# Down projections of an MLP as seven products of half blocks per pair of output tiles, in a two-layer streaming encoder on one core

## The chip, the cores and the metric

The kernel runs on one core of a Trainium2 chip. A core has five engines that work at the same time, each through its own queue of instructions, in order: TensorE (PE) multiplies matrices, VectorE (DVE), ScalarE (ACT) and GpSimd (POOL) work on elements, and SyncE (SP) issues DMAs. ACT and POOL can issue DMAs too. They share an on-chip memory, SBUF, of 128 partitions; TensorE writes its results to the banks of a second memory, PSUM, from where the others read them. An instruction waits at the head of its queue until the data that it reads is there and the buffer that it writes is free, and what stands behind it waits with it.

The metric is the time of one execution on the device in microseconds (us), the median over several runs.

## The reference

One inference step on T = 576 tokens: 512 of a new stream and 64 of a running one. The model has a width of 1024 and two layers. Layer 0 mixes tokens with causal means over windows, layer 1 with sparse attention: an indexer scores the keys, the best are chosen, and attention runs over these. Each layer ends in an MLP of 4096 hidden features, and normalisation by the root of the mean square stands ahead of each part:

```python
def _mlp(h, w_up, w_down):
    u = jax.nn.relu(h @ w_up)
    return (u * u) @ w_down

x = x + y.astype(x.dtype)
x = x + _mlp(_rmsnorm(x, norm_mlp[i]), mlp_w_up[i], mlp_w_down[i])
```

All is 32-bit floating point. The two MLPs have most of the multiplications: `w_up` is 1024 x 4096, `w_down` 4096 x 1024.

## The kernel before, in words

**Layout.** Activations lie with features on the partitions and tokens along the free axis. The residual stream `x` is eight tiles of 128 features by 576 tokens. A matmul takes a 128x128 block of weights, loaded into TensorE first (PEld in the profile), and streams tokens past it, half of them (`HT` = 288) at a time.

**Three passes.** Each float32 operand is taken apart into an upper part that TensorE takes as `fp32r` and a lower part, the rest. A product is then upper by upper, upper by lower and lower by upper: three matmuls in place of one. `project` (L151, the matmul at L159) does this for one output tile of 128 features: for each of eight k tiles, three passes over two halves of tokens, so 48 matmuls into two banks of PSUM.

**Weights.** They come as blocks of 128x1024, one for each output tile, in a list `blocks` in the order of use. `next_block` (L135) keeps two blocks ahead: it loads a block by a DMA on ACT's queue (`load`, L107; two raw tiles), and `split_weights` (L112) lets ACT write the upper part (L115) and DVE the lower one (L116) into one of three pairs of weight tiles.

**The MLP.** `mlp` (L245) takes the hidden features in four chunks of 1024. A chunk has an up stage of eight output tiles and a down stage of eight. After each up tile `squared` (L250) makes the factor of the down stage: DVE takes relu times 1/rms out of PSUM (L252), ACT squares (L253), and `split` makes the upper part on ACT (L145) and the lower on DVE (L146). A down tile sums over the eight factors of its chunk, and DVE adds it to the residual (L277). The last three tiles of the last chunk of layer 1 are done by `last` (L281) in two parts of the tokens, so that the final norm of the one runs beside the products of the other; this part alone has TensorE's order written out by hand.

**Norms.** `Norm` squares each tile of x on ACT, sums on DVE, and `stats` and `spread` sum over partitions by matmuls on TensorE (`st` in the profile, then `rb`, after a diagonal that DVE makes at L202). At the start of attention `split_x` (L236) makes the split activations `xs` of attention from x, tile by tile, and the norm's sums with them. The first products of attention are `ki` (the indexer's keys) and `pj` (projections, rotated by `rope`); `ki` is read by DVE at L609 and L610 once 1/rms is spread, since cosine and sine carry it.

**Order.** Outside of `last` a scheduler in the compiler of the kernel places the instructions on each engine, by the dependencies and by a model of the times. It may move the work of one stage beside that of another.

**Dependencies.** An engine waits for another by the tiles that both touch: a PSUM tile of two banks, as `ps` gives out (three buffers of them; `po` has two of one bank), is one tile for these waits.

## Time and profile before

| | |
|---|---|
| time, median of 3 runs | 1177.26 us (1177.13 to 1177.45) |
| the profiled execution: its span | 1175.3 us |
| TensorE matmuls busy, number | 1143.3 us, 97% of the span, 8580 |
| DVE busy | 595.4 us, 51% |
| ACT busy | 437.1 us, 37% |
| POOL busy | 169.1 us, 14% |
| DMA, mean over the span | 99 GB/s |

The span is the time from the first to the last instruction that the profiler recorded in one execution; the runs' time has about 2 us around it. Busy time is counted per engine. The page then shows the chain of work that ended last, followed back from the last instruction to what released it, step by step; groups of like instructions, with the busy time, the mean duration of one, and the idle time of the engine before them with what ended it; and the DMA issues with the median time from issue to landing. In a row `out<-in` names the tiles, `x384` counts instructions, and L159 is a line of the kernel. Two other views are rows in order of time (start, duration, engine, line) and tables of stretches of time (each engine's busy time, the clock that TensorE was granted, the share of the DMA engines, GB/s).

### The profile page before, as it was taken

The page shows a single profiled execution, that of the slowest core. Times are in us where ns is not written, and L with a number is a line of the kernel's source. Part 1 is how long each engine was busy: PE and PEld are TensorE (multiplying, and loading weights), DVE is VectorE, ACT ScalarE, POOL GpSimd, SP SyncE. Part 2 cuts the span into 40 slices and gives each one's busy share as a digit, 9 for nine tenths or more (in the row PEclk, how much of TensorE's full clock was granted, in tenths as well). Part 3 has the DMA queues.
Part 4 walks back from the last instruction along what each step waited for, and adds up shares of the span by engine and source line. Part 5 has one row for each costly group of instructions (what it writes and reads, how often), then busy time and mean ns, then how long its engine had stood idle before and what let it go on. Part 6 is the DMA issues. An engine that isn't in the chain of part 4 may idle for free.

```text
span 1175.3 us, 20225 instructions
## 1 busy us (share of the span) xinstructions
PE 1143.3 (97%) x8580; PEld 1130.9 (96%) x8580; DVE 595.4 (51%) x1000; ACT 437.1 (37%) x713; POOL 169.1 (14%) x125
## 2 busy tenths in 40 slices
PE   7999999999999999998889999999999999999996
PEld 6999999999999999998879999999999999999995
DVE  7844234333333445869999943753343334324444
ACT  5633123123212433344377665542133123213331
POOL 7600000000000000227874430000000000000002
PEclk8999999999999999999989999999999999999998
DMA  6222222222222233456452341422322222222212
GB/s 208 60 90 72 90 84 79 91 74 89 87 76 90 75 128 121 149 175 185 144 159 75 119 126 45 150 74 89 87 76 91 76 87 90 73 90 80 84 55 81
DMA packets 51146, 116.64 MB, mean 99 GB/s; under 512 B 9345, under 2 KB 22960, under 8 KB 51056
## 3 DMA queue, kind: packets, MB, share of 16 engines
q10 hardware_dynamic: 23184, 84.45, 23.2%
q1 hardware_dynamic: 27872, 30.90, 8.6%
q8 instruction: 67, 1.10, 0.4%
q14 instruction: 23, 0.19, 0.0%
HBM read 99.73 MB, written 13.25 MB: 96 GB/s over the span
## 4 chain that ended last, share of the span: by engine, by line
PE 90%; DVE 6%; ACT 1%; issue 1%; DMA 1%; SPq 0%; DVEq 0%; ACTq 0%
PE up L159 35%; PE dn L159 34%; PE pj L159 5%; PE o L798 2%; PE wa L159 2%; PE wo L159 2%; DVE work L723 1%; PE sc L759 1%; PE pt L779 1%; PE v L915 1%; PE pb L548 1%; DVE m L722 1%; DVE wl L116 1%; PE o L802 1%; PE z L441 1%
## 5 line engine op out<-in xcount | busy, mean ns | idle before, releaser
L115 ACT CAST wh<-raw 128x1024 fp32r<-128x1024 f32 (+1 forms) x161 | 168.8, 1049 | 603.9 <-PE dn L159 299.3
L159 PE MATMUL dn<-u,wh 128*128 128x288 f32 (+2 forms) x2048 | 358.2, 296 | 0.0
L159 PE MATMUL up<-xs,wh 128*128 128x288 f32 x2048 | 356.3, 296 | 0.0
L159 PEld LDWEIGHTS dn<-u,wh 128*128 128x128 f32 x2048 | 301.3, 188 | 0.2
L159 PEld LDWEIGHTS up<-xs,wh 128*128 128x128 f32 x2048 | 300.1, 188 | 0.2
L159 PE MATMUL dn<-u,wl 128*128 128x288 f32 (+2 forms) x1024 | 222.9, 295 | 0.0
L159 PE MATMUL up<-xs,wl 128*128 128x288 f32 x1024 | 219.0, 295 | 0.0
L116 DVE TENSOR_TENSOR wl<-raw,wh 128x1024 fp32r<-128x1024 f32 (+1 forms) x149 | 186.3, 1250 | 30.4 <-ACT wh L115 23.0
L277 DVE TENSOR_TENSOR x<-x,dn 128x576 f32<-128x576 f32 x61 | 46.0, 754 | 245.5 <-PE dn L159 245.5
L159 PEld LDWEIGHTS dn<-u,wl 128*128 128x128 f32 x1024 | 165.8, 188 | 0.0
L159 PEld LDWEIGHTS up<-xs,wl 128*128 128x128 f32 x1024 | 164.4, 188 | 0.1
L252 DVE SCALAR_TENSOR_TENSOR v<-up,rbm 128x576 f32<-128x576 f32 x64 | 48.3, 757 | 204.9 <-PE up L159 204.3
L159 PE MATMUL pj<-xs,wh 128*128 128x288 f32 x448 | 79.5, 296 | 0.0
L305 POOL TENSOR_TENSOR x<-x,rb 128x320 f32<-128x320 f32 (+1 forms) x9 | 7.9, 908 | 454.7 <-ACT rb L301 454.7
L159 PEld LDWEIGHTS pj<-xs,wh 128*128 128x128 f32 x448 | 66.5, 188 | 0.6
L606 POOL TENSOR_TENSOR cs<-cs,rba 128x576 f32<-128x576 f32 x1 | 1.9, 1862 | 415.2 <-ACT rba L190 415.2
L146 DVE TENSOR_TENSOR u<-v,u 128x576 fp32r<-128x576 f32 x64 | 48.4, 758 | 13.3 <-ACT u L145 13.2
L159 PE MATMUL pj<-xs,wl 128*128 128x288 f32 x224 | 48.4, 295 | 0.0
L738 ACT ACTIVATE p<-p,nm 128x128 f32<-128x128 f32 (+4 forms) x72 | 41.9, 584 | 10.4 <-DVE nm L737 10.1
L253 ACT ACTIVATE v<-v 128x576 f32<-128x576 f32 x64 | 43.9, 687 | 2.4 <-DVE v L252 1.9
L145 ACT CAST u<-v 128x576 fp32r<-128x576 f32 x64 | 43.1, 676 | 1.9
L798 PEld LDWEIGHTS o<-V,pT 128*128 128x128 f32 x320 | 40.2, 196 | 1.9 <-ACT pT L780 1.5
(191 smaller groups left out, 1215.4 us busy)
## 6 DMA issues: line engine op xcount, KB each, us to landing
raw<-in_w_up ACTq DMA_DIRECT2D x64, 512.0 KB, 3.6
raw<-in_w_down ACTq DMA_DIRECT2D x64, 512.0 KB, 3.5
raw<-in_w_o ACTq DMA_DIRECT2D x16, 512.0 KB, 3.6
raw<-in_w_in ACTq DMA_DIRECT2D x15, 512.0 KB, 3.9
q<-st SPq DMA_DIRECT2D x32, 144.0 KB, 2.5
q<-q SPq DMA_DIRECT2D x16, 256.0 KB, 2.8
x<-in_x SPq DMA_DIRECT2D x8, 288.0 KB, 5.9
xd<-x SPq DMA_DIRECT2D x4, 576.0 KB, 2.8
```

The costliest lines, as they stand in the source:

```text
L115: (act.copy if top is act else top.tensor_copy)(h[:, :n], raw[:, :n])
L116: sub.tensor_tensor(l[:, :n], raw[:, :n], f32(h[:, :n]), ALU.subtract)
L145: act.copy(dst[:, 0], src)
L146: sub.tensor_tensor(dst[:, 1], src, f32(dst[:, 0]), ALU.subtract)
L159: pe.matmul(pt[:, h, :m], wt[:, k * P:(k + 1) * P], xs[k][:, part, c:c + m], start=(k == 0 and i == 0), stop=(k == n - 1 and i == 2),)
L252: dve.scalar_tensor_tensor(halves(v), pt[:, :, :HT], 0.0, halves(norm.rb), ALU.max, ALU.mult)
L253: act.activation(v, v, AF.Square)
L277: dve.tensor_tensor(halves(x[m]), halves(x[m]), pt[:, :, :HT], ALU.add)
L441: pe.matmul(z[s, i][:n, (g % 2) * 256:(g % 2 + 1) * 256], lhs, rhs, start=kk + j == 0, stop=kk == 1 and j == 2)
L548: pe.matmul(pt[:, c0:c0 + rhs.shape[1]], lhs, rhs, start=n == 0, stop=n == len(steps) - 1)
L738: act.activation(dst, dst, AF.Exp, scale=-1.0, bias=nm, accum_out=sums)
L798: pe.matmul(oc[:, 2 * s + hh], pT[:, c:c + P], V[:, kt, vs], start=kt == 0, stop=kt == i)
```

## The change

The down stages of all four chunks of layer 0 and of the first three of layer 1 take two output tiles at a time and compute them by Strassen's scheme in Winograd's form. The two output tiles by two halves of k make a 2x2 block matrix of weights, a11 to a22 (128x512 each in the layout of the blocks), and the two halves of k by two halves of tokens one of factors, b11 to b22. Eight products of such blocks become seven, of weights a11, a12, a22 and four sums of weights with b11, b21, b22 and four sums of factors (t1 to t4). Each product is 12 matmuls: four k tiles, three passes, one half of the tokens.

- **Weights.** Blocks and pairs stand in one list `jobs`, and the generator `made` yields units of 128x512, upper and lower part each; an ordinary block is two units. There are six unit tiles, and two more (`more`) during the MLPs, every fourth unit from those two. Of a pair both blocks are loaded whole into `pair` tiles (one pair's worth of buffers). The sum s1 comes by a plain load of a quarter and an accumulating DMA on POOL's queue, the sum with a21 by another such DMA into the raw tile; the two values of s2 come by POOL additions. `next_unit` keeps four more units ahead.
- **Factors.** After two up tiles (the order of the up tiles, `UP_ORDER`, pairs k with k + 4) `factors` makes four sums on DVE and splits seven factors in four wide instructions.
- **Products.** `Pair` has banks a and b, halves of one PSUM tile, and c, a tile by itself. Three products open the pair, each into a bank of its own; four more go on accumulating into a, b, c and b, and after each DVE adds that bank to the residual (the line after `product` in `closing`). The first product, a11 by b11, is needed in all four outputs: it is summed over the chunks in `part_sums` and added on POOL in the last Strassen chunk.
- **Order.** TensorE's order in both MLPs is that of the source (`manual_schedule`); the first up tile of the next chunk stands ahead of a down stage. In the first pair of a chunk the last quarter of the three opening products runs after the first three quarters of all three.
- **Memory.** Tile pools that were there for the whole kernel are now opened for each stage (`stage`).

The pool mixer's weights and the value projection's are cut into units as well. The core of the diff:

```diff
-SLOTS = {"x": 4, "xs": 8, "a": 3, "b": 3, "c": 3, "d": 3, "e": 2}
+SLOTS = {"xs": 8, "a": 3, "b": 3, "c": 3, "d": 3, "e": 2}
+UNITS = 6
+UP_ORDER = (0, 4, 1, 5, 2, 6, 3, 7)
+FACTORS = ("b11", "b22", "b21", "t1", "t2", "t3", "t4")
...
-    weights = ctx.enter_context(tc.tile_pool(name="weights", bufs=3))
+    weights = ctx.enter_context(tc.tile_pool(name="weights", bufs=UNITS))
...
+    @contextmanager
+    def stage(**pools):
+        with ExitStack() as st:
+            phase.clear()
+            for name, bufs in pools.items():
+                phase[name] = st.enter_context(tc.tile_pool(name=uid(name), bufs=bufs, reuse_waits="tile"))
+            yield
...
+    def mlp_jobs(layer, strassen):
+        for c in range(4):
+            ups = [("block", a["w_up"][layer, c * 8 + f], KT * P) for f in UP_ORDER]
+            jobs.extend(ups[1:] if c else ups)
+            if c < 3:
+                jobs.append(("block", a["w_up"][layer, (c + 1) * 8 + UP_ORDER[0]], KT * P))
+            if c < strassen:
+                jobs.extend(("pair", a["w_down"][layer, c, 2 * q], a["w_down"][layer, c, 2 * q + 1]) for q in range(KT // 2))
+            else:
+                jobs.extend(("block", a["w_down"][layer, c, m], KT * P) for m in range(KT))
...
+    def unit(n=512):
+        extra = phase.get("more")
+        count[0] += 1
+        if extra and made_units[0] % 4 == 3:
+            got = [extra.tile([P, 528], F32R, tag=t, bufs=2, name=uid(t)) for t in ("wh", "wl")]
+        else:
+            got = [weights.tile([P, 528], F32R, tag=t, name=uid(t)) for t in ("wh", "wl")]
+        made_units[0] += 1
+        return [t[:, :n] for t in got]
...
+    def split_unit(src, n=512):
+        h, l = unit(n)
+        act.copy(h, src)
+        how["sub"].tensor_tensor(l, src, f32(h), ALU.subtract)
         return h, l
...
+    def made():
+        while jobs:
+            kind, one, two = jobs.pop(0)
+            if kind == "block":
+                raw = load(one, two, act)
+                for i in range(2):
+                    yield split_unit(raw[:, i * two // 2:(i + 1) * two // 2], two // 2)
+                continue
+            r = [phase["pairs"].tile([P, KT * P], F32, tag="pair", bufs=2, name=uid("pair")) for _ in range(2)]
+            for t, src in zip(r, (one, two)):
+                act.dma_start(t, src)
+            a11, a12, a21, a22 = (t[:, i * 512:(i + 1) * 512] for t in r for i in range(2))
+            s1, s2 = (phase["pairs"].tile([P, 512], F32, tag="sum", bufs=4, name=uid("sum")) for _ in range(2))
+            act.dma_start(s1, two[:, :512])
+            pool.dma_start(s1, two[:, 512:], accum_op=ALU.add)
+            pool.dma_start(a21, one[:, :512], accum_op=ALU.add)
+            pool.tensor_tensor(s2, s1, a11, ALU.add)
+            yield split_unit(a11)
+            yield split_unit(s2)
+            yield split_unit(s1)
+            yield split_unit(a12)
+            yield split_unit(a21)
+            pool.tensor_tensor(s2, s2, a12, ALU.add)
+            yield split_unit(s2)
+            yield split_unit(a22)
...
+    def next_unit(ahead=4, sub=dve):
+        how["sub"] = sub
+        while len(ready) <= ahead:
+            u = next(units, None)
...
+        return ready.pop(0)
...
+        def factors(v):
+            t = phase["acts"].tile([P, 4, HT], F32, tag="t", bufs=1, name=uid("t"))
+            u = phase["u"].tile([P, 7, 2, HT], F32R, tag="u", bufs=4, name=uid("u"))
+            b12, b11, b22, b21 = (v[:, i] for i in range(4))
+            act.copy(u[:, 0:3, 0], v[:, 1:4])
+            dve.tensor_tensor(t[:, 0], b11, b12, ALU.subtract)
+            dve.tensor_tensor(t[:, 1], b22, t[:, 0], ALU.add)
+            dve.tensor_tensor(t[:, 2], b12, b22, ALU.subtract)
+            dve.tensor_tensor(t[:, 3], b21, t[:, 1], ALU.subtract)
+            act.copy(u[:, 3:7, 0], t)
+            dve.tensor_tensor(u[:, 0:3, 1], v[:, 1:4], f32(u[:, 0:3, 0]), ALU.subtract)
+            dve.tensor_tensor(u[:, 3:7, 1], t, f32(u[:, 3:7, 0]), ALU.subtract)
             return u
...
+        def product(bank, w, us, factor, js, first, last):
+            for j in js:
+                wh, wl = (t[:, j * P:(j + 1) * P] for t in w)
+                uh, ul = (us[j][:, FACTORS.index(factor), i] for i in range(2))
+                for i, (wt, ut) in enumerate(((wh, uh), (wh, ul), (wl, uh))):
+                    pe.matmul(bank[:, :HT], wt, ut, start=first and j == 0 and i == 0, stop=last and j == 3 and i == 2,
+                              skip_group_check=True)
...
+                ab = psum("ab")
+                self.a, self.b, self.c_ = ab[:, 0], ab[:, 1], psum1("c")
+                self.lo, self.hi = ([x[2 * q + i][:, c0:c0 + HT] for i in range(2)] for c0 in (HT, 0))
...
+            def opening(self, parts=((0, 1, 2, 3),)):
+                ws = [next_unit() for _ in range(3)]
+                for js in parts:
+                    for w, bank, factor in zip(ws, (self.a, self.b, self.c_), ("b11", "t2", "t1")):
+                        product(bank, w, self.us, factor, js, True, True)
+                    yield
+                self.opened()
...
+            def opened(self):
+                q = self.q
+                if self.c == 0:
+                    part_sums[q] = phase["acts"].tile([P, HT], F32, tag=f"g{q}", bufs=1, name=uid("g"))
+                    act.copy(part_sums[q], self.a[:, :HT])
+                else:
+                    dve.tensor_tensor(part_sums[q], part_sums[q], self.a[:, :HT], ALU.add)
+                dve.tensor_tensor(self.hi[0], self.hi[0], self.b[:, :HT], ALU.subtract)
+                dve.tensor_tensor(self.hi[1], self.hi[1], self.c_[:, :HT], ALU.subtract)
+                if self.c == strassen - 1:
+                    g = part_sums[q]
+                    pool.tensor_tensor(self.hi[0], self.hi[0], g, ALU.add)
+                    pool.tensor_tensor(self.hi[1], self.hi[1], g, ALU.subtract)
+                    pool.tensor_tensor(self.lo[1], self.lo[1], g, ALU.subtract)
...
+            def closing(self):
+                js = (0, 1, 2, 3)
+                for bank, factor, out, b2 in ((self.a, "b21", self.lo[0], 0), (self.b, "t3", self.hi[1], 0),
+                                              (self.c_, "b22", self.hi[0], 0), (self.b, "t4", self.lo[1], 0)):
+                    product(bank, next_unit(), self.us, factor, js, False, True)
+                    dve.tensor_tensor(out, out, bank[:, :HT], ALU.add)
...
+        def down(c, us):
+            for q in range(KT // 2):
+                p = Pair(c, q, us)
+                for _ in p.opening(((0, 1, 2, 3),) if q else ((0, 1, 2), (3,))):
+                    pass
+                p.closing()
...
+        steps = [s for c in range(4) for s in [(c, i) for i in range(c > 0, 8)] + ([(c + 1, 0)] if c < 3 else []) + [(c, None)]]
+        for n, (c, i) in enumerate(steps):
+            if i is not None:
+                w = next_block(sub=add if n < 2 else dve)
                 pt = psum("up")
                 project(pt, w, xs)
...
+            if c < strassen:
+                down(c, us[c])
+                continue
...
-    pool_mixer()
-    mlp(0, 1, ["xs"] * KT, "abcdabcdabcd", pool)
-    attention()
-    mlp(1, 3, "aaabbbcc", ["xs"] * KT + ["c", "d", "d", "d"], end=last)
+    x = Residual()
+    with stage(slots=1, xs=1, tmps=6):
+        pool_mixer()
+    with stage(u=1, xs=1, acts=1, tmps=3, pairs=1, more=2):
+        with tc.manual_schedule(engines={ENG.PE}):
+            mlp(0, 1, 4, pool)
+    with stage(slots=1, xs=1, cst2=1, tmps=6):
+        attention()
+    with stage(xs=1, u=1, acts=1, tmps=3, pairs=1, more=2):
+        with tc.manual_schedule(engines={ENG.PE}):
+            mlp(1, 3, 3, end=last)
```

More of the change, by code (lines that the diff above doesn't have):

```diff
@@ L1 @@
-from contextlib import ExitStack
+from contextlib import ExitStack, contextmanager
 import numpy as np
@@ L126, in pool_dsa_kernel @@
[L126 to L140 removed]
+    jobs = []
@@ L532, in pool_mixer @@
             dve.tensor_copy(sband, sraw)
-            src, n = blocks.pop(0)
-            split_blocks.append(split_weights(load(src, n, act), n, act, pool))
+            how["sub"] = pool
+            for _ in range(2):
+                ready.append(next(units))
         two = psum("z")
```

155 lines of the change are left out of this document (87 added, 68 removed).

## The prediction

> **What bounds the kernel now.** I read the page first: busy time, chain, groups.
>
> ```profile
> span 1175.3 us, 20225 instructions
> PE 1143.3 (97%) x8580; PEld 1130.9 (96%) x8580; DVE 595.4 (51%) x1000; ACT 437.1 (37%) x713; POOL 169.1 (14%) x125
> PE 90%; DVE 6%; ACT 1%; issue 1%; DMA 1%; SPq 0%; DVEq 0%; ACTq 0%
> L115 ACT CAST wh<-raw 128x1024 fp32r<-128x1024 f32 (+1 forms) x161 | 168.8, 1049 | 603.9 <-PE dn L159 299.3
> ```
>
> TensorE is 97% busy and makes 90% of the chain; ACT's idle time is waiting for TensorE. Then the chain in order of time, where the down and up stages stand as unbroken pieces:
>
> ```profile
> 101.84 50.96 PE dn L159 x384
> 152.80 51.01 PE up L159 x384
> 458.68 6.39 PE ki L159 x48
> 465.19 0.99 PE st L209 x10
> 466.19 6.46 PE pj L159 x47
> 472.64 0.97 PE rb L189 x4
> ```
>
> A down stage is 384 matmuls in 50.96 us, 132.7 ns each, without a gap, and attention's first products follow without one. In the MLP the time is the number of matmuls; anything that makes TensorE wait there is added to the span. The table of stretches for a down stage says what room the others have:
>
> ```profile
> 100.00:150.00 50.00, 50.00 (x379) 50.00 (x378) 16.60 (x17) 9.76 (x10) 0.00 (x0) 1.00 0.26 78
> ```
>
> DVE is a third busy, ACT a fifth, POOL idle, the granted clock full.
>
> The profiled span is 1175.3 us and the runs' median 1177.3; I carry the 2.0 us around the span through unchanged and make the sum on the span.
>
> **What is removed.** A pair of output tiles takes 96 matmuls now (2 tiles x 8 k x 3 passes x 2 halves), 84 as seven products of 12. Four chunks of layer 0 and three of layer 1, four pairs each: 28 x 12 = 336 matmuls less, x 132.7 ns = **-44.6 us**. All matmuls of a product go to one bank; that costs nothing by the attention's output products, which do so already:
>
> ```profile
> 636.55 2.85 PE wa L159 x24
> ```
>
> 24 of 256 columns in 2.85 us are 119 ns, 107 of streaming and 12 over; 132.7 for 288 columns is 120 and 12.7.
>
> **New waits of TensorE inside a pair.** The products run a(b11), b(t2), c(t1), a(b21), b(t3), c(b22), b(t4); call them 1 to 7. Banks a and b are halves of one tile, and the changed program waits by tile: product 5 starts only when DVE has read a after product 4, and nothing stands between the two. Product 4 waits in the same way for DVE's reading of b after product 2; product 7 for that of product 5, with product 6 between. The price of such a wait is the drain, the reading, and the restart:
>
> ```profile
> 394.56 0.43 PE L159 MATMUL up<-xs,wl 128*128 128x288 f32 x2
> 394.82 0.56 PE L159 MATMUL up<-xs,wh 128*128 128x288 f32 x3
> 395.02 0.76 DVE L252 SCALAR_TENSOR_TENSOR v<-up,rbm 128x576 f32<-128x576 f32 x1 [3.41 <-PE up L159]
> L327 DVE TENSOR_TENSOR x<-x,dn x6: 407/455/489, 1144.1 to 1162.1; 128x320 f32<-128x320 f32 x3, 128x256 f32<-128x256 f32 x3
> 8.79 1.23 DVE L417 TENSOR_TENSOR wl<-raw,wh 128x1024 fp32r<-128x1024 f32 x1 [1.38 <-ACT wh L414]
> 10.07 0.19 PEld L441 LDWEIGHTS z<-wl,xs 128*128 128x128 f32 x1 [0.48 <-DVE wl L417]
> ```
>
> The next block's first matmul takes its place at 394.82, DVE reads the old one at 395.02: 0.20. Reading 128x288 lies between the 407 and 489 ns of 256 and 320 columns: 0.45. DVE ends at 10.02, the weight load starts at 10.07, its matmul some 0.04 later: 0.09. Together 0.74 us before product 5 of every pair. In the last pair of layer 0 the scheduler has put attention's products into the gaps, so 27 x 0.74 = **+20.0**. Bounds: 0, if the reading were somehow covered, and 27 x 1.2 = 32, if DVE is late by one subtraction.
>
> Before product 4 the readings of a and b (0.45 each) have one product, 1.59 us, to hide under in an ordinary pair. Not in the first pair of a chunk, where the last quarter of products 1 to 3 runs together: 0.8 us in five chunks. In each layer's first chunk ACT copies a, behind the copy of a weight, and DVE's reading of b stands behind it (in the first pair behind a subtraction and c's reading too): about 1.9 us in its first pair, 0.4 in the three others. 5 x 0.8 + 2 x 1.9 + 6 x 0.4 = **+10.2** (0 to 15).
>
> **Engines beside it.** Weights are split in units of 512 columns, seven per pair in place of two blocks of 1024.
>
> ```profile
> L145 ACT CAST ck<-raw 128x512 fp32r<-128x512 f32 x4 | 2.5, 622 | 2.2 <-DMA raw<-in_cache_k 2.2
> L146 POOL TENSOR_TENSOR ck<-raw,ck 128x512 fp32r<-128x512 f32 x4 | 5.2, 1293 | 12.6 <-ACT ck L145 6.6 <-issue 6.0
> L116 DVE TENSOR_TENSOR wl<-raw,wh 128x1024 fp32r<-128x1024 f32 x54 | 66.2, 1226 | 9.1 <-ACT wh L115 6.0
> L146 DVE TENSOR_TENSOR u<-v,u 128x576 fp32r<-128x576 f32 x30 | 22.7, 758 | 6.3 <-ACT u L145 6.3
> ```
>
> A subtraction of 512 columns is 0.69 by the line through 576 and 1024. Per pair, 11.15 us of matmuls and some 12 with the waits: ACT 7 x 0.62 = 4.4; DVE 7 x 0.69 + 8 x 0.45 = 8.4; POOL 2 x 1.3, two DMA issues, and three 128x288 additions in the closing chunk. All fit, so they cost nothing as busy time; if that cover went, DVE would bind first, at 1.4 times its load. Up stages: two blocks cost DVE 2 x 0.76 + 4 x 0.45 + 1.1 + 1.4 for the factors and 4 x 0.69 for weights, 8.6 of 12.7 us, also nothing. The last factors are ready 6.3 us after the last block and the next chunk's first block, put between, gives 6.4.
>
> POOL beside DVE does cost:
>
> ```profile
> L149 DVE SCALAR_TENSOR_TENSOR xs<-x,gv,xs x7: 803/1267/2062, 40.4 to 53.1; 128x576 fp32r<-128x576 f32 x7
> L556 DVE SCALAR_TENSOR_TENSOR x<-pb,gv,x x6: 804/806/818, 39.6 to 51.5; 128x576 f32<-128x576 f32 x6
> ```
>
> Between 40 and 53 us, POOL busy, an operation with two inputs from SBUF went from 803 to 2062 ns, one with an input from PSUM stayed at 804 to 818. So the readings keep their price and the subtractions queued before them may be half as long again while a POOL addition runs. One addition falls on the subtraction ahead of product 4's reading: I take 0.1 us a pair, **+3** (0 to 15).
>
> **The accumulating DMAs.** No DMA of POOL's queue is in this trace. The nearest rows:
>
> ```profile
> raw<-in_w_down ACTq DMA_DIRECT2D x64, 512.0 KB, 3.5
> raw<-in_cache_k SPq DMA_DIRECT2D x4, 256.0 KB, 2.6
> V<-in_cache_v SPq DMA_DIRECT2D x1, 512.0 KB, 6.2
> ```
>
> One accumulation moves 256 KB and reads 256 KB more: between 2.6 and 6.2 us from landing to landing; I take 4.3, the 3.5 of 512 KB with 0.8 for POOL's wake-up and issue. It matters in one place. The raw tiles hold one pair, so the second load of pair q+1 waits for the last subtraction of pair q, 1.5 us after product 6 of pair q-1. Then 3.5 load, the accumulation, 0.72 copy, 0.75 subtraction; and that subtraction stands on DVE's queue ahead of the reading that product 7 of pair q waits for. 1.5 + 3.5 + A + 1.5 must be within 12.0 - 0.65 = 11.35 us, so A up to about 4.7 (4.6 over a chunk's three handovers) is free, and each us above costs about 2 us a chunk, 14 in all. At 4.3: **+2** for the loads that collide (0 to 22 at 6.2). ACT, which issues the loads, waits there too, but its next copy waits for the same data. The sum by DMA goes earlier (two pairs ahead) and is covered.
>
> [...]
>
> **Entry to attention.** Now the squares and sums of the attention norm are made tile by tile under the down products; with the change the queues hold all seven after the last residual. In the changed order TensorE runs ki, pj, pj, then the sums st, then rb, then a pj whose bank ki's rope must free.
>
> ```profile
> 468.61 0.25 DVE L202 TENSOR_SCALAR diag<-ident,r 128x64 f32<-128x64 f32 x1
> 477.31 0.76 DVE L610 TENSOR_TENSOR t<-ki,sn 64x576 f32<-64x576 f32 x1
> ```
>
> From the end of st (466.2) to the diagonal 2.7 us; from rb's start (472.64) to the end of ki's reading 5.4, of which rb is 1.0. Now both lie beside products; then TensorE stands 2.7 + 4.4 = 7.1. The sums come late as well: ACT's squares stand behind a weight copy that waits for a unit of six to be free, and DVE's last two additions behind a weight loaded only after those squares. I count 17 us after the last down product against 12 of TensorE work left: 5. Together **+12** (5, if the norm is on time and half the rest is absorbed, to 15). Later, eight weight blocks between the top-k steps cost DVE 2 x 0.69 - 1.23 = 0.15 more: **+1**.
>
> **Sum.** -44.6 + 20.0 + 10.2 + 3 + 2 + 12 + 1 = +3.6; 1177.3 + 3.6 = **1181 us**. From no change a measurement of this kernel tells about 0.2%, 2.4 us.
>
> **Rivals.** (1) *The entry to attention is free.* If ropes and index scores have slack for the late norm, 12 goes: 1169. For it: that stage waits on DVE later anyhow. Against: TensorE ran without a gap there until 505 us. It ends on the faster side once 6 of the 12 are absorbed. (2) *The bank waits are hidden*, DVE's reading overlapping the next product: 20 less, 1161, or 1151 with product 4's. Against: nothing stands between products 4 and 5. [...] (3) *The accumulations set the pace*: at A = 6.2, 1203; it decides from 4.6 us. For it: an unmeasured path through POOL, two of them per pair. Against: 256 KB in 2.6 us. A change that does nothing is excluded: the matmul count falls.
>
> **Chances.** Forecast, 1172 to 1191 by itself, 0.43; rival 1 0.20; rival 2 0.12; rival 3 0.22; other 0.03. The forecast's lower end and rival 1's upper give 0.11 for within 0.2%, so faster 0.33, slower 0.56. Range 1156 to 1204: the low end cuts the whole of rival 2's best case, the high end takes rival 3 at 6.2.
>
> **What would show it.** Matmuls down by 336. A down stage of some 48 to 51 us instead of 50.96; in it a gap of TensorE of 0.74 us before each product 5, released by DVE's reading at the line that adds a bank to x. If that gap is absent, rival 2. Accumulations landing within 4.6 us and no wait of TensorE before product 7; otherwise rival 3. About 12 us of idle TensorE between the last down product and the values' product, released by DVE's sums and ki's rope. The prediction fails most if DVE's queue is late elsewhere, as a chain of blocked subtractions would show in stretches where POOL is busy.

## The result and the profile after

The changed kernel takes **1221.53 us** (median of 4 runs, 1219.73 to 1224.47) against 1177.36 before: a ratio of 1.038, 95% interval 1.036 to 1.040. It is slower by 44 us where 4 were forecast, and lies 17 us above the range. The profiled execution has a span of 1222.7 us, 47.4 more than before.

The page of the changed kernel: busy time, chain, the subtractions that read a pair (busy, mean ns | idle before, and what ended it), and the accumulating DMAs (KB, median us to landing).

```profile
span 1222.7 us, 20812 instructions
...
PE 1125.7 (92%) x8244; PEld 1102.5 (90%) x8244; DVE 816.9 (67%) x1478; ACT 534.4 (44%) x968; POOL 314.8 (26%) x274
...
PE 77%; DVE 11%; issue 5%; ACT 3%; DMA 3%; POOL 1%; SPq 0%; DVEq 0%; ACTq 0%; POOLq 0%
...
L167 DVE TENSOR_TENSOR wl<-pair,wh 128x512 fp32r<-128x512 f32 x112 | 104.0, 929 | 50.8 <-ACT wh L166 49.1
...
pair<-in_w_down POOLq DMA_DIRECT2D x28, 256.0 KB, 4.1
sum<-in_w_down POOLq DMA_DIRECT2D x28, 256.0 KB, 5.3
```

And from its groups by line, the products into banks a and b, with all that ended TensorE's idle time before them:

```profile
L357 PE MATMUL ab<-u,wh 128*128 128x288 f32 x1120 | 236.5, 305 | 50.3 <-DVE x L397 39.8 <-DVE x L384 9.3 <-DVE u L349 1.0
```

The matmuls are 336 fewer, as forecast, but TensorE's share of the chain fell from 90% to 77%, and DVE's rose from 6% to 11%. TensorE stood 39.8 us before products 5 and 7 and 9.3 before product 4. A subtraction of a pair's quarter took 929 ns in the mean, where 690 were worked out.

The table of stretches has the down stages of layer 0 and of layer 1's Strassen chunks (time, then busy time and instructions of PE, PEld, DVE, ACT and POOL, granted clock, DMA share, GB/s):

```profile
116.60:170.40 53.80, 47.55 (x338) 45.80 (x337) 32.77 (x53) 18.90 (x34) 13.95 (x13) 0.97 0.56 137
221.30:271.75 50.45, 45.95 (x338) 44.67 (x338) 33.66 (x56) 17.48 (x30) 13.95 (x13) 1.00 0.59 146
322.60:373.90 51.30, 45.98 (x338) 44.68 (x338) 34.63 (x56) 16.80 (x28) 13.86 (x13) 1.00 0.59 144
418.30:476.00 57.70, 47.66 (x314) 46.33 (x313) 44.84 (x61) 22.92 (x35) 21.11 (x23) 0.88 0.42 118
841.00:897.30 56.30, 48.03 (x339) 46.17 (x339) 32.31 (x52) 18.00 (x32) 13.81 (x13) 0.97 0.55 132
948.00:999.30 51.30, 46.00 (x339) 44.71 (x338) 34.39 (x57) 17.72 (x30) 14.09 (x13) 1.00 0.55 143
1050.00:1110.90 60.90, 50.30 (x338) 49.22 (x337) 42.11 (x56) 18.33 (x31) 21.67 (x21) 0.92 0.34 84
```

A stage that needs 44.6 us took 50.5 to 60.9; one before took 50.96. (The row of layer 0's closing chunk ends with 295 of its 336 matmuls begun, as attention's first products run between the last ones.) The middle chunks, 50.5 to 51.3 us, are about where the forecast put them, at 48 to 51. The first chunk of each layer and above all the closing ones (418 and 1050) are not, and in just those the granted clock is under 1. What happens there is seen in order of time, around the second pair of the closing chunk of layer 0: first TensorE, DVE and POOL (start, duration, line; in brackets the idle time before and what ended it),

```profile
438.19 4.04 DVE L167 TENSOR_TENSOR wl<-pair,wh 128x512 fp32r<-128x512 f32 x1
442.15 0.44 DVE L397 TENSOR_TENSOR x<-x,ab 128x288 f32<-128x288 f32 x1
437.27 0.86 POOL L188 DMA_DIRECT2D pair<-in_w_down  x1 [2.58 <-DVE x L384]
437.83 1.61 POOL L195 TENSOR_TENSOR sum<-sum,pair 128x512 f32<-128x512 f32 x1
439.09 1.10 POOL L390 TENSOR_TENSOR x<-x,g 128x288 f32<-128x288 f32 x1
439.83 1.09 POOL L388 TENSOR_TENSOR x<-x,g 128x288 f32<-128x288 f32 x1
440.58 1.08 POOL L389 TENSOR_TENSOR x<-x,g 128x288 f32<-128x288 f32 x1
442.74 0.82 PE L357 MATMUL ab<-u,wh 128*128 128x288 f32 x2 [3.49 <-DVE x L397]
```

then stretches of 2 us with TensorE alone (busy, matmuls, granted clock, DMA share, GB/s):

```profile
442.00:444.00 2.00, 1.26 (x5) 0.50 0.34 72
446.00:448.00 2.00, 2.00 (x10) 0.50 0.00 0
450.00:452.00 2.00, 2.00 (x17) 1.00 0.55 80
```

POOL has four additions queued behind an accumulating DMA, and when that is issued they run one after the other. DVE's subtraction of two tiles in SBUF, 0.69 us elsewhere, starts beside the first and ends after the last, 4.04 us later. Behind it stands the reading of bank a, and for that product 5 waits 3.49 us. In this execution four rows of additions in the closing chunks stand directly behind a DMA issue, and each held a subtraction so, for 4.04 to 4.76 us. Beside the four rows of additions with no issue directly ahead of them no subtraction took over 1.75 us. Then the clock is halved for over 6 us: 10 matmuls in 2 us in place of 17. I summed this over both executions in stretches of 1 us, busy time times what the clock is short of 1: **27.4 us after, 7.7 before**.

The last unforeseen piece is the norm of the first MLP, again in order of time:

```profile
55.34 3.88 POOL L253 TENSOR_TENSOR s<-s,sq 128x576 f32<-128x576 f32 x2
60.93 2.17 PE L285 MATMUL st<-ones,s 128*128 128x2 f32 x10 [5.75 <-DVE s L253]
```

The sums of squares on POOL end so late that TensorE stands 5.75 us and then runs slowly; before, they began at 41.8 and TensorE passed without a gap.

So the 47.4 us are, from the rows of TensorE in order of time (gaps over 0.15 us): -44.6 for the matmuls, +37.2 before product 5, +9.3 before product 4, +2.6 before product 7, +5.8 in the norm of the first MLP, +8.2 at the entry to attention, +1.3 at two smaller places, +19.7 for the clock. That is 39.5. Most of the rest goes to restarts: by the starts of the matmuls a gap drawn as 0.64 us sets the work back by 0.87, so some forty gaps cost 0.2 each beyond what is drawn.

### The profile page after: what moved, and what is told of

Read it like the earlier page. It is cut to its first block, busy times and chain, and to the rows that moved or that the text cites. A ratio compares the mean times of both kernels' runs of the same rounds, so it can differ in the third digit from the quotient of the medians.

```text
span 1222.7 us, 20812 instructions
## 1 busy us (share of the span) xinstructions
PE 1125.7 (92%) x8244; PEld 1102.5 (90%) x8244; DVE 816.9 (67%) x1478; ACT 534.4 (44%) x968; POOL 314.8 (26%) x274
## 4 chain that ended last, share of the span: by engine, by line
PE 77%; DVE 11%; issue 5%; ACT 3%; DMA 3%; POOL 1%; SPq 0%; DVEq 0%; ACTq 0%; POOLq 0%
PE up L235 32%; PE ab L357 15%; PE c L357 6%; PE pj L235 5%; DVE wl L167 4%; PE dn L235 4%; PE o L972 2%; PE wo L235 2%; PE wa L235 2%; DMA pair<-in_w_down 2%; PE sc L933 1%; ACT wh L166 1%; PE v L1089 1%; PE pt L953 1%; DVE work L897 1%
## 5 line engine op out<-in xcount | busy, mean ns | idle before, releaser
L357 PE MATMUL ab<-u,wh 128*128 128x288 f32 x1120 | 236.5, 305 | 50.3 <-DVE x L397 39.8
L357 PEld LDWEIGHTS ab<-u,wh 128*128 128x128 f32 x1120 | 184.1, 194 | 60.2 <-issue 19.7
L166 ACT CAST wh<-raw 128x512 fp32r<-128x512 f32 (+1 forms) x210 | 128.4, 620 | 234.5 <-PE up L235 99.7
L167 DVE TENSOR_TENSOR wl<-raw,wh 128x512 fp32r<-128x512 f32 (+1 forms) x186 | 139.4, 754 | 76.2 <-ACT wh L166 74.6
L357 PE MATMUL ab<-u,wl 128*128 128x288 f32 x560 | 168.6, 301 | 0.0
L167 DVE TENSOR_TENSOR wl<-pair,wh 128x512 fp32r<-128x512 f32 x112 | 104.0, 929 | 50.8 <-ACT wh L166 49.1
L195 POOL TENSOR_TENSOR sum<-sum,pair 128x512 f32<-128x512 f32 x28 | 39.2, 1400 | 296.6 <-DVE wl L167 296.6
L357 PEld LDWEIGHTS ab<-u,wl 128*128 128x128 f32 x560 | 108.5, 194 | 0.0
L357 PE MATMUL c<-u,wh 128*128 128x288 f32 x448 | 94.6, 304 | 0.0
L189 POOL TENSOR_TENSOR sum<-sum,pair 128x512 f32<-128x512 f32 x28 | 38.5, 1373 | 155.8 <-DMA pair<-in_w_down 148.2
L357 PEld LDWEIGHTS c<-u,wh 128*128 128x128 f32 x448 | 75.3, 197 | 0.0
```

The costliest lines, as they stand in the source:

```text
L166: act.copy(h, src)
L167: how["sub"].tensor_tensor(l, src, f32(h), ALU.subtract)
L189: pool.tensor_tensor(s2, s1, a11, ALU.add)
L195: pool.tensor_tensor(s2, s2, a12, ALU.add)
L357: pe.matmul(bank[:, :HT], wt, ut, start=first and j == 0 and i == 0, stop=last and j == 3 and i == 2, skip_group_check=True)
```

## The experiments

Three causes stood to be told apart: the shared tile of banks a and b, DVE held up by POOL, and the accumulating DMAs (rival 3); and the price of a long gap had to be measured by itself. Ratios are to the kernel before on the same chip, with their 95% intervals; the change itself stands at 1.038.

**Banks apart.**

```diff
-                ab = psum("ab")
-                self.a, self.b, self.c_ = ab[:, 0], ab[:, 1], psum1("c")
+                self.a, self.b, self.c_ = psum1("a"), psum("b")[:, 0], psum("c")[:, 0]
```

> The changed kernel with banks a, b and c of a pair in three PSUM tiles of their own; nothing else is changed. Theory (product 5 waits for a reading that it doesn't need, since a and b are one tile; DVE's late readings then slow the clock): the gaps of TensorE before product 5 (37 us drawn) are gone, those before product 4 mostly, and with them some 13 us of slow clock; 1221.5 - 37 - 7 (restarts) - 6 - 13 = about 1160 us, between 1152 and 1175, and no gap of TensorE in a down stage is longer than 2 us. Rival (DVE as a whole is too late, whatever it reads): the same gaps stand before product 6 or 7 instead, and the time stays above 1200.

1185.3 us (1177.2 to 1194.3), ratio 1.007 (1.004 to 1.010): 36 us of the expected 61. The gaps before product 5 are gone, but there are new ones, 23.8 us before product 7, and single gaps of up to 4.4 us. The group of bank b in its groups by line, and then its chain at one of these gaps (start, duration, what):

```profile
L357 PE MATMUL b<-u,wh 128*128 128x288 f32 x672 | 140.8, 302 | 25.4 <-DVE x L396 23.8 <-DVE u L349 1.0 <-ACT wh L166 0.6
```

```profile
336.29 4.28 DMA pair<-in_w_down
...
341.12 5.81 DMA pair<-in_w_down
...
349.01 0.45 DVE x L396
```

The load of the next pair's block and the accumulation onto it, 4.28 and 5.81 us, stand one behind the other. Then come copy and subtraction, and behind that subtraction on DVE's queue the reading that product 7 waits for. This is rival 3's chain. In the change, where TensorE comes later to product 7, only 2.6 us of it showed.

**POOL's additions left out, and accumulations left out** (each from the changed kernel).

```diff
-            pool.tensor_tensor(s2, s1, a11, ALU.add)
...
-            pool.tensor_tensor(s2, s2, a12, ALU.add)
...
-                    pool.tensor_tensor(self.hi[0], self.hi[0], g, ALU.add)
-                    pool.tensor_tensor(self.hi[1], self.hi[1], g, ALU.subtract)
-                    pool.tensor_tensor(self.lo[1], self.lo[1], g, ALU.subtract)
```

> The changed kernel without POOL's additions: s1 is used where s2 is wanted, and the three additions of the first product's sums in the closing chunk are left out. The output is not the reference's; loads, accumulating DMAs, splits and matmuls stay as many. Theory (a subtraction of DVE that starts beside a POOL addition lasts until POOL is done, and the reading behind it is late): every subtraction takes 0.69 us, every gap before product 5 is 0.55 to 0.65 us, 21 us less than now, and some 10 us of slow clock go; about 1190 us, between 1183 and 1198. Rival (DVE is late by its own load or by the loads of weights): less than 6 us faster, 1215 or more.

1193.4 us, ratio 1.014 (1.012 to 1.016): as expected. The subtractions are all as worked out, at 690 ns, and the gaps before product 5 (L393) and 4 (L382) are what the shared tile alone makes: 16.6 us before product 5 in place of 37.2. The clock costs 19.4 us in place of 27.4. Its groups by line:

```profile
L167 DVE TENSOR_TENSOR wl<-pair,wh 128x512 fp32r<-128x512 f32 x112 | 77.2, 690 | 58.6 <-ACT wh L166 56.8
L355 PE MATMUL ab<-u,wh 128*128 128x288 f32 x1120 | 232.7, 301 | 25.9 <-DVE x L393 18.0 <-DVE x L382 6.3 <-DVE u L347 1.0
```

```diff
-            pool.dma_start(s1, two[:, 512:], accum_op=ALU.add)
-            pool.dma_start(a21, one[:, :512], accum_op=ALU.add)
```

> The changed kernel without the two accumulating DMAs of a pair: s1 is its first quarter alone and a21 stays as loaded, so the output is not the reference's; all else stays. Theory (accumulations are nearly hidden): the gaps before product 7 (2.6 us) go, and what POOL's issues take from the sums of the first MLP norm, 2 us; 1217 us, between 1210 and 1221. Rival (the third one of the prediction, accumulations set the pace): 1206 or less.

1201.0 us, ratio 1.019 (1.015 to 1.022): 20 us faster, the rival's side. Yet only 2.6 us of gaps stood before product 7. The gaps of 3.5 and 4.2 us before product 5 in the closing chunk of layer 0 are 0.7 to 0.8 here, those of 3.8 and 3.2 us in layer 1 are 0.64. The same four additions still run one after the other, but now DVE gets through between them (POOL, then DVE's subtractions):

```profile
435.23 1.29 POOL L193 TENSOR_TENSOR sum<-sum,pair 128x512 f32<-128x512 f32 x1 [3.99 <-DVE wl L167]
436.48 1.26 POOL L388 TENSOR_TENSOR x<-x,g 128x288 f32<-128x288 f32 x1
437.70 1.24 POOL L386 TENSOR_TENSOR x<-x,g 128x288 f32<-128x288 f32 x1
438.90 0.81 POOL L387 TENSOR_TENSOR x<-x,g 128x288 f32<-128x288 f32 x1
435.79 1.27 DVE L167 TENSOR_TENSOR wl<-sum,wh 128x512 fp32r<-128x512 f32 x1
437.35 0.93 DVE L167 TENSOR_TENSOR wl<-pair,wh 128x512 fp32r<-128x512 f32 x1
```

So a row of additions alone does not hold DVE for its whole length, and neither does a DMA issue alone: without the additions every subtraction took 0.69 us. It takes both, an issue and additions directly behind it. In the 17 traces of this case all 25 subtractions of a quarter or a sum that took over 1.9 us (up to 4.76) run beside an addition directly behind an issue; without accumulating DMAs none took over 1.8. Product 5 waits 15.5 us less in this run, so most of the 20 us come by what the issues do on POOL, not by when the accumulations land. What passes between POOL and DVE there, the traces don't show.

**Gaps put in on purpose** (the kernel before, TensorE in source order).

```diff
+    def gap(src):
+        g = tmp("gap")
+        dve.tensor_tensor(g, src, src, ALU.add)
+        for _ in range(gaps[0] % 7):
+            dve.tensor_tensor(g, g, g, ALU.min)
+        gaps[0] += 1
+        pe.matmul(psum1("gp")[:, :2], g[:, :P], ones[:, :2], start=True, stop=True)
```

> The kernel before, with TensorE in source order in the MLPs and 28 gaps put in on purpose, one after every second down tile of seven chunks: TensorE waits for DVE's reading of the tile and a chain of 1 to 7 steps of DVE. Theory (a gap above some 2.5 us halves the granted clock for a few us): gaps up to 2 us cost their length, those of 3.5 us and more cost 1.4 to 3 us on top, with a granted clock of 0.50 in the rows right behind them; those between sometimes. Rival (the clock falls for another reason, such as the number of short gaps): the granted clock stays 1.00 behind these gaps, as no stage is short of work.

> The kernel before with 28 gaps on purpose as in the earlier kernel with gaps, but with steps of 128x144 on DVE: gaps from some 0.7 us to some 3.3 us. Theory (the clock falls when TensorE idles for most of some fixed stretch of 2 to 3.5 us): no slow rows behind gaps under 1.5 us, 1.7 us lost behind most of those over 2.2 us, either between. Rival (each wait, however short, costs clock): slow rows behind the shortest gaps too.

The first kernel takes 1389.9 us (ratio 1.180), the second 1358.0 (1.155). In the second `g` is cut to 144 columns and the steps are doubled. Its gaps are 1.19, 2.88 and from 3.57 us up. Two of them in order of time, and then the stretches behind them with TensorE alone:

```profile
131.75 0.38 PE L253 MATMUL gp<-ones,gap 128*128 128x2 f32 x2 [2.89 <-DVE gap L251]
148.57 0.59 PE L253 MATMUL gp<-ones,gap 128*128 128x2 f32 x2 [3.57 <-DVE gap L251]
```

```profile
131.80:138.20 6.40, 6.40 (x49) 1.00 0.28 82
148.60:152.00 3.40, 3.40 (x14) 0.50 0.41 147
152.00:155.40 3.40, 3.40 (x19) 0.62 0.00 0
```

Behind the four gaps of 1.19 and the three of 2.88 us the clock stays full; behind all twenty of 3.57 to 6.9 us it is halved, and 1.7 to 3.2 us are lost on top, no more behind the longest than behind the shortest. Below 3.4 us it goes both ways: in the first kernel three of four gaps of 1.64 us lost 1.7 us, in the changed kernel gaps of 2.47 and 2.82 us did, one of 2.15 did not.

The clock's record in the traces shows what decides. In each of the 17 traces the granted clock changes only on a grid of 3.41 us. Here it is 0.50 from 147.75 to 154.58, from 168.23 to 175.06 and from 239.91 to 246.74: two steps each, with starts 6 and 21 steps apart. I added up TensorE's idle time in every step that ran at full clock, leaving out the first 30 and the last 5 us of each trace. All 135 steps with more than 1.86 us were followed by a step at 0.50; of some 5400 with less, 19 were, 15 of these with 1.4 us or more. So a gap counts by how much of it lies within one step: the three of 2.88 us lie across two, with at most 1.85 us in one, and that of 2.47 us lies in one. Of the four gaps of 1.64 us the one that cost nothing lies across two, the others in one.

The second kernel's theory is borne out, with a stretch of 3.41 us; the first one's lower bound, 2 us, is not: gaps from 1.64 us on can cost the clock as well.

**Strassen switched off**, all else of the change kept.

```diff
-            mlp(0, 1, 4, pool)
+            mlp(0, 1, 0, pool)
...
-            mlp(1, 3, 3, end=last)
+            mlp(1, 3, 0, end=last)
```

> The changed kernel with Strassen in no chunk: all down tiles are plain products, while pools by stage, units of 512 columns and TensorE's order from the source stay. Theory (part of the loss has nothing to do with Strassen: the squares of the first MLP norm start late in pools opened for the stage, 8 us with the slow clock behind it, and the norm of attention is late, some 5): 1190 us, between 1183 and 1198. Rival (all of the loss is made in the seven products): between 1175 and 1181.

1181.9 us, ratio 1.006 (1.003 to 1.008), a little under the theory's range and above the rival's. The norm of the first MLP waits here too, 5.84 us, though this kernel has no accumulating DMA, and is most of it. At the entry to attention there is no gap over 0.2 us: those come with the seven products.

**What the waits before product 7 are.** Banks apart, and no accumulations:

> The kernel with banks apart, and without the two accumulating DMAs (its output is not the reference's: s1 is its first quarter, a21 as loaded). Theory (with banks apart the gaps before product 7, 24.4 us drawn, come from the chain of load and accumulation of the next pair): they are gone, with some 4 us of restarts and 6 of slow clock; 1185.3 - 34 = 1151 us, between 1144 and 1159. Rival (these gaps come from POOL's additions beside DVE): less than 10 us faster, 1175 or more.

1152.8 us, ratio 0.980 (0.978 to 0.982): as expected. Then two thirds of that gain without leaving anything out, by loads that can start earlier (smaller raw tiles, another order and SP's queue, which this run does not tell apart):

```diff
-            r = [phase["pairs"].tile([P, KT * P], F32, tag="pair", bufs=2, name=uid("pair")) for _ in range(2)]
-            for t, src in zip(r, (one, two)):
-                act.dma_start(t, src)
-            a11, a12, a21, a22 = (t[:, i * 512:(i + 1) * 512] for t in r for i in range(2))
+            a11, a12, a21, a22 = (phase["pairs"].tile([P, 512], F32, tag=t, bufs=1, name=uid(t)) for t in ("a11", "a12", "a21", "a22"))
...
-            act.dma_start(s1, two[:, :512])
+            for t, src in ((a11, one[:, :512]), (s1, two[:, :512]), (a21, two[:, :512]), (a12, one[:, 512:]), (a22, two[:, 512:])):
+                nc.sync.dma_start(t, src)
```

> The kernel with banks apart; the raw tiles of a pair are four quarters of 128x512 in place of two blocks, loaded by SP's queue in the order a11, first part of s1, a21, a12, a22, so that a21's load waits for the fifth subtraction of the pair before and not for the last, and no wait of a load stands on ACT's queue. Nothing is left out. Theory (lead of the accumulation is what is short): a21 is ready some 4 us earlier; gaps before product 7 fall from 24 us to under 6; 1185.3 - 18 - 3 - 5 = 1159 us, between 1150 and 1170. Rival (POOL's own path is the limit, its issues wait for its additions): 1178 or more.

1164.5 us, ratio **0.990** (0.988 to 0.992): now faster than before. The idle time of bank b's matmuls, in this kernel's groups by line, is down to a quarter:

```profile
L355 PE MATMUL b<-u,wh 128*128 128x288 f32 x672 | 137.4, 296 | 6.7 <-DVE x L394 5.8 <-DVE u L347 0.9
```

In its chain the second down stage of layer 0 lies between the ends of up work at 213.34 and the start of up work at 258.39: 45.05 us where the matmuls need 44.6 and the changed kernel took 50.45.

> As the one before (banks apart, quarters on SP's queue), with the additions of s2 and of the first product's sums on DVE in place of POOL. Theory (POOL's additions hold subtractions of DVE up, and DVE has room: 34 of 51 us in a down stage, with 5.5 us more in a stage and 3.6 in a closing one): 3 to 8 us faster than it, about 1154. Rival (an addition in DVE's queue that waits for an accumulation blocks the readings of banks behind it): 5 us slower than it or more.

1166.3 us, ratio 0.992 (0.990 to 0.993), no different from the one before. The gain was not there: the subtractions are all short, but readings of a, b and c now wait in DVE's own queue, 0.2 to 0.6 us at a dozen places. Nor was the rival's loss. So in this kernel the additions cost as much in DVE's queue as on POOL.

> The changed kernel with the quarters of a pair loaded by SP's queue, and banks a and b in one tile as in the change. Theory (two causes that are separate: the shared tile makes product 5 wait for the late reading, the short lead makes the accumulation late): the gaps before product 5 stay, with an accumulation that POOL issues earlier and so with fewer additions in a bunch; about 1205 us, between 1195 and 1214, against 1221.5 with neither and 1164.5 with both. Rival (lead is all, and banks only hide it): below 1180.

1206.7 us, ratio 1.027 (1.024 to 1.031): as the theory has it. Earlier loads alone bring 15 us, banks apart alone 36, both 57. The accumulating DMAs are all there, but none is issued directly ahead of a row of additions: no subtraction takes over 1.84 us, and no gap before product 5 is over 1.8.

**The norms** (`add` on DVE in the first MLP; then attention's squares and sums behind each pair of the last down stage).

```diff
-            mlp(0, 1, 4, pool)
+            ahead = []
+            mlp(0, 1, 4, dve, then=ahead)
...
+                if then is not None and c == 3:
+                    if q == 0:
+                        then.append(Norm("a"))
+                    for k in (2 * q, 2 * q + 1):
+                        then[0].add(k)
```

> Banks apart and quarters on SP's queue, and the sums of the first MLP norm, with the splits of the first two blocks, on DVE in place of POOL. Theory (the norm's 7.9 us gap and 4 us of slow clock come from POOL's sums of 1.4 to 2.1 us, which stand between POOL's issues and additions): the gap shrinks to under 3 us; 1164.5 - 8 = 1156 us, between 1152 and 1161. Rival (the squares on ACT start too late, and the engine of the sums doesn't matter): within 2 us of 1164.5.

1160.3 us, ratio 0.986 (0.984 to 0.988). The gap is 4.5 us in place of 7.9, and the slow clock behind it stays, 3.8 us: half of the theory's gain, since the squares come late as well: ACT begins to square the later tiles at 45.6 us, in the kernel before at 39.6.

> As the one before, and the squares and sums of attention's norm made in the last down stage of layer 0, two tiles after each pair, in that stage's own buffers. Theory (the norm at the entry is late because its squares are queued behind weight splits that wait for TensorE): the gap of 2.7 us before the spread and most of the 4.1 us before the third projection go, with 3 us of slow clock; 1156 - 7 = 1149 us, between 1144 and 1154. Rival (cosine, sine and rope take these 4 us whenever the norm is ready): less than 3 us faster than it.

1158.0 us, ratio 0.985 (0.984 to 0.987). The gaps of 2.7 and 4.1 us at the entry are one of 1.24, but the time is only 2 us lower, by the letter the rival's result. So the late norm is what made these gaps. In the profiled executions a gap before a product 7 in the closing chunk, 1.4 us in the one, is 2.8 in the other, with a slow clock behind it, so that part of what was gained is lost there.

**Which of POOL's additions, and is the clock a cost of its own?**

```diff
-                    pool.tensor_tensor(self.hi[0], self.hi[0], g, ALU.add)
+                    dve.tensor_tensor(self.hi[0], self.hi[0], g, ALU.add)
```

(and the two lines below it)

> The changed kernel with only the three additions of the first product's sums, in the closing chunks, on DVE in place of POOL; both sums of s2 stay on POOL. Theory (four POOL additions in a row hold one subtraction for 4 us, and such a gap costs the clock as well): the gaps before product 5 in the closing chunks (0.8 to 4.2 us, 19 in all) fall to 1 to 2 us, some 9 us, and 8 to 10 us of slow clock go; 1221.5 - 18 = 1203 us, between 1196 and 1209. Rival (the sums of s2 alone do it, in all chunks): less than 6 us faster.

1215.3 us, ratio 1.034 (1.030 to 1.039): 6 us, at the rival's edge, and the interval overlaps that of the change. The gaps of the closing chunks fell by 5 us and not by 9, as a DMA issue with one addition of s2 behind it is enough to hold DVE up. Here it holds one of the additions moved over, 0.45 us elsewhere, for 2.09 us (DVE, then POOL):

```profile
440.88 2.09 DVE L389 TENSOR_TENSOR x<-x,g 128x288 f32<-128x288 f32 x1
442.89 0.44 DVE L397 TENSOR_TENSOR x<-x,ab 128x288 f32<-128x288 f32 x1
440.49 0.86 POOL L188 DMA_DIRECT2D pair<-in_w_down  x1 [5.73 <-DVE x L385]
441.05 1.59 POOL L195 TENSOR_TENSOR sum<-sum,pair 128x512 f32<-128x512 f32 x1
```

So rows and single additions both count, and neither alone is the cause.

```diff
+                    if factor == "b21" and self.c == strassen - 1 and self.q in (1, 2):
+                        idle = psum1("idle")
+                        product(idle, w, self.us, factor, js, True, True)
+                        product(idle, w, self.us, factor, (0, 1), True, True)
```

> The changed kernel with 18 matmuls into a bank of their own, which nobody reads, put in right behind product 4 in the second and third pair of both closing chunks, where TensorE stands 3.2 to 4.2 us; they take 2.4 us. The wait for DVE stays as it is. Theory (the slow clock behind a long gap is a cost of its own): gaps of 0.8 to 1.8 us are left, the clock stays at 1.00, and 3.0 + 2.4 + 1.7 + 1.7 us of slow clock are saved; 1221.5 - 8 = 1213 us, between 1209 and 1216. Rival (the clock costs nothing here, since DVE sets the pace): 1220 or more.

1219.1 us (1217.0 to 1221.0), ratio 1.036 (1.034 to 1.038) against 1.038: by the total the two cannot be told apart. In the traces the stretch itself is shorter: in layer 1's closing chunk, from the first product 4 to the last product 5, it is 46.5 us against 50.6, with a full clock. These are its first and last rows, of the changed kernel

```profile
1055.33 0.53 PE L357 MATMUL ab<-u,wh 128*128 128x288 f32 x2 [0.51 <-DVE x L384]
1105.94 0.51 PE L357 MATMUL ab<-u,wh 128*128 128x288 f32 x2 [0.64 <-DVE x L397]
```

and of this one:

```profile
1052.54 0.53 PE L357 MATMUL ab<-u,wh 128*128 128x288 f32 x2 [0.51 <-DVE x L384]
1099.08 0.50 PE L357 MATMUL ab<-u,wh 128*128 128x288 f32 x2 [0.64 <-DVE x L402]
```

Some 1.6 of these 4.1 us are luck: they were lost in the changed kernel to the slow clock behind the first pair's gap of 2.47 us, where nothing was put in. Here that gap is 2.45 us and lies across two steps of the clock's grid, with 1.56 us in one. The other 2.5 us were gained with 36 matmuls of no use added to the chunk, where 3.4 us of slow clock were to be saved. Elsewhere in that execution a late accumulation made a new gap of 2.99 us with a slow clock behind it. That the clock has a price is shown by the gaps put in on purpose; that the whole kernel gains by filling them is not.

> The kernel with banks apart, quarters on SP's queue and both norms on DVE, with the three closing additions on DVE as well. Theory (with banks apart and the accumulation early no reading waits long enough for the burst to matter): within 3 us of 1158. Rival (the burst still delays product 7 in the closing chunks, 1.3 and 2.8 us and a slow clock behind): 1153 or less.

1155.2 us (1152.6 to 1156.6), ratio **0.981** (0.980 to 0.983): the fastest with nothing left out, 1.9% under the kernel before, and 2.7 us below the one with the additions on POOL, just at the edge between theory and rival.

## Why the prediction was wrong, step by step

- **Matmuls, -44.6 us: right.** 8244 against 8580, and stages without waits run at 1.59 us a product.
- **POOL beside DVE, +3 (0 to 15): wrong, and the step that failed first.** Without the additions the kernel is 28 us faster: 20.6 us of the waits before product 5 go and 8.0 of slow clock. I took one addition a pair to lengthen one subtraction by half. The rows that I read (803 against 2062 ns) were right for what they showed, additions with no DMA issue ahead of them; but an accumulating DMA issued on POOL's queue directly ahead of additions makes one subtraction last up to 4.76 us, and the subtractions that read a pair took 929 ns in the mean for 690. The kernel before has no DMA on that queue, so no row of it could show this.
- **Product 5, +20.0 (0 to 32): the mechanism right, the size by that step wrong.** Nothing stands between products 4 and 5, and banks apart took the gaps away. Without POOL's additions the 27 gaps are 16.6 us drawn, and an undisturbed one sets the work back by 0.87 us where 0.74 was worked out. But 37.2 us are drawn: the bound "if DVE is late by one subtraction", 1.2 us a pair, did not hold.
- **Product 4, +10.2: right,** 9.3 drawn.
- **Accumulations, +2: right for the wait that I priced** (2.6 us before product 7; landing 4.1 us after the issue for a21, up to 6.6). The 0.8 us that I put down for POOL was an estimate that no row of before shows; in the change the issue for a21 occupies POOL for 0.86 us. By its own terms the time that is free is 11.35 - 6.5 = 4.85 us, not 4.7; nothing hangs on it. **Wrong as a whole:** without them the kernel is 20 us faster, because their issue, beside the additions, holds DVE up. With banks apart the chain of load and accumulation became the wait, 23.8 us drawn. Rivals 2 and 3 were not alternatives but stood one behind the other.
- **Entry to attention, +12 (5 to 15): right in kind.** 8.2 us drawn. That 2.9 of slow clock, which no term had, brings it near 12 is luck. With the seven products off there is no gap there, and with the norm made earlier one of 1.24 us is left; that the late residuals delay the norm is the likely link, but no run changes them alone.
- **Left out: the first MLP's norm,** 5.8 us and 2.7 of slow clock. I took this stage to be untouched. It is not POOL's queue of DMAs that does it: with the seven products off, and so no accumulating DMA, the wait is 5.84 us, and without the accumulations 5.63. The squares on ACT come later than before, and sums on DVE still leave 4.5 us; what in the new order of the stage delays them stays open.
- **Left out: the clock,** 19.7 us, about half of the 40 us missed; 8.0 of it are counted in POOL's 28 already. The traces of before showed it, a granted clock of 0.50 behind the gap of 5.87 us at 584 to 590 us, and I read only that it was full in the MLP. How much is lost depends on where each gap lies on the grid of 3.41 us, which lay differently from trace to trace.

The rival that came nearest was the third, at 1203, and for another reason than it gave: the accumulations cost time by their issue, not by landing late.

## What to carry to other kernels

When TensorE has no slack, ask of each new wait what stands ahead of the releasing instruction on its queue, and what can stretch that: here a DMA issue and additions on POOL, for which TensorE never waits directly, set how long it stood. Waits are not additive: a gap that leaves TensorE idle for over 1.86 us of a step of 3.41 us costs 1.2 to 3.3 us more by the clock in these runs, and removing one wait exposes the next in the same chain, so work out the second as well before choosing which to remove. The saving of an algorithm with fewer products came out only when accumulators that are read at different times had tiles of their own, and raw tiles were small enough to be reloaded as soon as each quarter was used.

## What the runs showed of the hardware that I had not expected

- A DVE subtraction with two inputs in SBUF took 0.69 us alone or beside a DMA issue of POOL alone, up to 1.84 beside POOL additions, and up to 4.76 beside additions directly behind a DMA issue. Between the additions of such a row it did not end: 4.04 us beside four of them. DVE's readings of a bank took 0.44 to 0.46 us beside an addition as elsewhere. A DVE addition with two inputs in SBUF, 0.45 us elsewhere, took 2.09 us beside a POOL addition of 1.59 us directly behind an issue.
- The granted clock changes on a grid of 3.41 us, and was 0.50 for one to three steps behind every step at full clock that left TensorE idle for over 1.86 us (135 of 135 in 17 traces). With the gaps put in on purpose the loss is 1.5 to 3.3 us whether the gap is 3.4 us or 8.
- An accumulating DMA of 256 KB on POOL's queue lands 4.1 to 5.3 us after its issue in the median, up to 7.4, and the issue occupies POOL for 0.88 us.
